# Two transfers in Pool's queue make one weight sum, and eighteen of twenty-two chunk pairs take seven products

## The chip, the cores and the metric

The kernel runs on one core of one Trainium2 chip. The metric is the device time of a run in microseconds; lower is better. The core has TensorE (PE, matrix products), VectorE (DVE), ScalarE (ACT) and GpSimd (Pool) for work on tiles, and SyncE (SP), which here only issues transfers. Each engine runs its own list of instructions in order and waits on semaphores for the others. Transfers run beside the engines on 16 DMA engines.

## The reference, cut to what matters

Two layers, each of a feed-forward network (FFN), a token mix with three kinds of attention, and another FFN, each followed by a layer norm. The change touches the first half of the FFNs only:

```python
def _swiglu(x, w1, w2):
    gt, up = jnp.split(x @ w1, 2, axis=-1)
    return (jax.nn.silu(gt) * up) @ w2
...
for l in range(DEPTH):
    x = _layer_norm(DN_ALPHA * x + 0.5 * _swiglu(x, ffn1_w1[l], ffn1_w2[l]), ln1_g[l], ln1_b[l])
    mix = _token_mix(x, w_in[l], ...)
    x = _layer_norm(DN_ALPHA * x + mix, ln2_g[l], ln2_b[l])
    x = _layer_norm(DN_ALPHA * x + 0.5 * _swiglu(x, ffn2_w1[l], ffn2_w2[l]), ln3_g[l], ln3_b[l])
```

All is fp32. There are 512 tokens of width 1024, and the hidden width is 2816, so that `w1` has 1024 x 5632 elements: 22 chunks of 128 gate columns, then 22 chunks of 128 up columns.

## The kernel before, in words

**Precision.** An fp32 operand is split into a rounded part `hi` and the rest `lo`. A product takes three matmuls: `hi` with the high part of the tokens (`xh`), `hi` with the low part (`xl`), and `lo` with `xh`. The split of a weight tile (`wsplit`, L146 and L147) is a copy on ACT, which makes `hi`, and a subtraction on DVE, which makes `lo`.

**Pairs.** An FFN works through 22 pairs f = 0 to 21, pair f being gate chunk f and up chunk f. Pairs 0 and 1 are `staged`: their weights come ahead of time, and their products run while the layer norm before them is ending. The others run in the loop in `ffn`. There are four FFNs in a run, which are called FFN0 to FFN3 here in order of time; FFN0 and FFN1 belong to the first layer.

**Plain pairs.** The pairs in `PLAIN` (0, 1, 2, 3, 4, 5 and 14) load two raw tiles of 512 KB (`wcols`), split both, and run two products of 8 steps of k with three matmuls of 128x512 each (`proj`, `mm3`, L167 to L169).

**Short pairs.** The other fifteen pairs go through `seven` and `strassen`. The gate and up columns of a chunk, each cut in two halves of k, form a 2 x 2 block matrix, and the tokens, cut in halves of k and of the 512 tokens, another. Their product takes seven block products instead of eight, which needs sums of weight blocks and sums of token blocks. A block product is four steps of k with three matmuls of 128x256 (L357). `seven` loads the raw tiles `rg` and `ru` in SP's queue (L286, L287) and makes four sums of 128x512 on DVE: L293 `x1[h1] = ru[h1] + ru[h2]`, L294 `x1[h2] = x1[h1] - rg[h1]`, L295 `x2[h1] = rg[h1] - ru[h1]`, L296 `x2[h2] = rg[h2] - x1[h2]`. Then `x1`, `x2` and half of `ru` are split (L298 on ACT and L299 on DVE for the first two, L300 and L301 for the half, into `dh` and `dl`), and `rg` is split by `wsplit`. The token sums are made once in each FFN (`token_sums`, L314 to L320), after pair 2. `strassen` gathers the results from PSUM with five DVE rows of 128x256 (L368 to L376), and `evac` applies the gate with a tanh on ACT and two DVE rows of 128x512 (L335, L336).

**Buffers.** Raw tiles share three buffers (tag `raw`). `x1` and `x2` share the tag `ws` with two buffers. `dh` and `dl` have one each. The split tiles go round a fixed rotation in `unit`: three buffers in `wt`, twice two in `more`, twice two in `w1p`; a counter runs on from FFN to FFN. `evac` has three buffers `t`.

**Order.** PE and Pool run in the order of the program text (`manual_schedule`). The instructions of ACT, DVE and SP are put in order by a scheduler. Pool's queue holds in each FFN the four stores of the residual `x_sp` (L382) at the start and its four loads `xa` (L415) after the loop, and between FFNs arithmetic of the layer norm and the attention.

**Around it.** In FFN0 two transfers of 1.5 MB (`bvec`) are issued in the loop. After the loop, the second weight `w2` is multiplied row by row (`rows_ln`), with the layer norm at its end.

Of the kernel before, what the change touches and what calls it, by code (L numbers as in the profile page):

```python
# [9 lines left out]
F32 = mybir.dt.float32  # L10
# [3 lines left out]
OP = mybir.AluOpType  # L14
# [4 lines left out]
P = 128  # L19
S, D, F = 512, 1024, 2816  # L20
KD, KF, NB = D // P, F // P, S // P
# [43 lines left out]
def body(tc, a, out, depth=DEPTH):  # L65
    nc = tc.nc
# [48 lines left out]
    def wraw(shape=None):  # L115
        return wt.tile(list(shape or [P, KD, P]), F32, name="raw", tag="raw", bufs=3)
# [11 lines left out]
    nx = K()  # L128
    nx.pool = nx.w1 = None

    def unit():

        if nx.pool:
            pl, nb = nx.pool, 4
        else:
            seq = [(wt, 3)] * 3 + [(more.pool, 2)] * 2 * bool(more.pool) + [(nx.w1, 2)] * 2 * bool(nx.w1)
            more.n += 1
            pl, nb = seq[more.n % len(seq)]
        return [pl.tile([P, KD, P], F32R, name=n, tag=n, bufs=nb) for n in ("hi", "lo")]

    def wsplit(raw, n=KD, step=None):
        hi, lo = unit()
        step = step or n
        for i in range(0, n, step):
            c = slice(i, i + step)
            nc.scalar.activation(hi[:, c], raw[:, c], AF.Copy)  # L146
            nc.vector.tensor_tensor(lo[:, c], raw[:, c], hi[:, c].bitcast(F32), op=OP.subtract)  # L147
        return hi, lo
# [123 lines left out]
        return pts  # L272

    NTAIL = 4
    PLAIN = (0, 1, 2, 3, 4, 5, 14)

    def ffn_first(w1):
        return [wcols(w1, c) for c in (0, F, P, F + P)]
# [1 line left out]
    def seven(w1, f):  # L280

        v = w1.rearrange("(k p) f -> p k f", p=P)
        rg, ru = wraw(), wraw()
        nc.sync.dma_start(rg, v[:, :, f * P:(f + 1) * P])  # L286
        nc.sync.dma_start(ru, v[:, :, F + f * P:F + (f + 1) * P])  # L287
        ug, u1, u2 = wsplit(rg), unit(), unit()
        ud = [nx.w1.tile([P, 4, P], F32R, name=n, tag=n) for n in ("dh", "dl")]
        h1, h2 = slice(0, 4), slice(4, 8)  # L290
        x1, x2 = [nx.w1.tile([P, KD, P], F32, name="ws", tag="ws", bufs=2) for _ in range(2)]
        tt = nc.vector.tensor_tensor
        tt(x1[:, h1], ru[:, h1], ru[:, h2], op=OP.add)  # L293
        tt(x1[:, h2], x1[:, h1], rg[:, h1], op=OP.subtract)  # L294
        tt(x2[:, h1], rg[:, h1], ru[:, h1], op=OP.subtract)  # L295
        tt(x2[:, h2], rg[:, h2], x1[:, h2], op=OP.subtract)  # L296
        for (hi, lo), x in ((u1, x1), (u2, x2)):
            nc.scalar.activation(hi, x, AF.Copy)  # L298
            tt(lo, x, hi.bitcast(F32), op=OP.subtract)  # L299
        nc.scalar.activation(ud[0], ru[:, h2], AF.Copy)  # L300
        tt(ud[1], ru[:, h2], ud[0].bitcast(F32), op=OP.subtract)  # L301
        return ug, u1, u2, ud
# [20 lines left out]
    def ffn(l, w1, w2, which, xap, xa, wts, pend, done_prev, last, nxt):  # L323


        st = K()
        NA = KF - NTAIL

        def hpart(f):
            return (st.ha, st.hb)[f >= NA][:, f - NA * (f >= NA)]  # L330

        def evac(f, pg, pu):
            t = st.lnp.tile([P, S], F32, name="t", tag="t", bufs=3)
            nc.scalar.activation(t, pg, AF.Tanh, scale=0.5)
            nc.vector.scalar_tensor_tensor(t, t, 1.0, pg, op0=OP.add, op1=OP.mult)  # L335
            nc.vector.tensor_tensor(hpart(f), t, pu, op=OP.mult)  # L336
# [10 lines left out]
        def strassen(f, ws):  # L347
            (ug, u1, u2, ud), (t1, t2, t3, t4) = ws, st.t
            ga, pa, pb = ps(name="pg"), ps(name="pu"), ps(name="pv")
            p_, r_, s_ = [(xh[:, k:k + 4, c], xl[:, k:k + 4, c]) for k, c in ((0, H1), (4, H1), (4, H2))]  # L350

            def prod(o, w, k0, x, first=True):
                for k in range(4):
                    hi, lo = w[0][:, k0 + k], w[1][:, k0 + k]
                    vh, vl = x[0][:, k], x[1][:, k]
                    for i, (wx, vx) in enumerate(((hi, vh), (hi, vl), (lo, vh))):
                        nc.tensor.matmul(o, wx, vx, start=first and k == 0 and i == 0, stop=k == 3 and i == 2,  # L357
                                         skip_group_check=True)

            tt = nc.vector.tensor_tensor  # L360
            prod(ga[:, H1], ug, 0, p_)
            prod(ga[:, H2], u1, 0, t1, False)
            sn = st.w1p.tile([P, S], F32, name="sn", tag="sn", bufs=2)
            nc.scalar.activation(sn, ga, AF.Copy)
            prod(pa[:, H1], u1, 4, t2)
            prod(pa[:, H2], u2, 0, t3, False)
            v = st.w1p.tile([P, S], F32, name="v", tag="v", bufs=2)
            tt(v[:, H1], pa[:, H1], sn[:, H1], op=OP.add)  # L368
            tt(v[:, H2], pa[:, H2], v[:, H1], op=OP.add)
            prod(pb[:, H1], ud, 0, t4)  # L370
            u = hpart(f)
            tt(u[:, H1], pb[:, H1], v[:, H2], op=OP.add)
            tt(u[:, H2], sn[:, H2], v[:, H2], op=OP.add)
            prod(ga[:, H1], ug, 4, r_, False)
            prod(ga[:, H2], u2, 4, s_, False)
            tt(ga[:, H2], ga[:, H2], v[:, H1], op=OP.add)  # L376
            evac(f, ga, u)

        pts = staged(wts, pend)
# [8 lines left out]
        st.ha = fa.tile([P, NA, S], F32, name="ha")  # L388
        st.w1p = nx.w1 = pool("w1p", side="right", reuse_waits="tile")
        evac(0, pts[0], pts[1])  # L390
        evac(1, pts[2], pts[3])
        for f in range(2, KF):
            if after and f in (10, 14):
                i = after.pop()
                nc.sync.dma_start(bvec[i], bsml[i, :, None, :].to_broadcast([H, P, TLEN]))
            if f == KF - 1:
                for k, n in enumerate(("hi", "lo")):
                    h_parts(k, wt.tile([P, KD, P], F32R, name=n, tag=n, bufs=3)
                            .rearrange("p (a b) c -> p a (b c)", a=2))
            if f not in PLAIN:  # L400
                strassen(f, seven(w1, f))
                continue
            wg, wu = wcols(w1, f * P), wcols(w1, F + f * P)
            pg, pu = ps(name="pg"), ps(name="pu")
            proj(pg, wg)
            proj(pu, wu)
            evac(f, pg, pu)
            if f == 2:
                token_sums(st)
# [952 lines left out]
```

## Time and profile before

| | |
|---|---|
| median of the runs | 2524.89 us |
| lowest and highest | 2524.28 and 2526.05 us |
| profiled execution | 2527.23 us |
| its span on the core | 2525.5 us |
| mean granted clock of PE | 0.995 |
| busy: PE, DVE, ACT, Pool | 98%, 64%, 43%, 8% |
| DMA, SP's queue and Pool's queue | 35.3% and 2.2% of the 16 engines' time |

The span runs from the first to the last instruction of the profiled execution. Names such as `L357` are lines of the kernel file. In a row of the profile `out<-in` gives the tiles by the names of the program, and x24 says that 24 instructions stand in one row. "Idle before" is the time that an engine stood still just before a row, with the engine and instruction that released it. PEclk is the clock that was granted to PE, 1.00 being full speed.

### The profile page before, as it was taken

The numbers are of one execution on the slowest core, as the hardware profiler recorded it, in microseconds if no ns is written. First come the engines' busy times: TensorE is split into PE (matmuls) and PEld (weight loads), VectorE is DVE, ScalarE is ACT, GpSimd is POOL, SyncE is SP. The second block draws the span as 40 slices with busy tenths as digits, with TensorE's granted clock in tenths as the row PEclk, the third lists the DMA queues.
The fourth block names the chain that finished last, engine by engine and source line by source line (L and its number), as shares of the span: only waits on it lengthen the run. The fifth ranks groups of instructions, "written<-read, shape, count | busy, mean of one in ns | idle before, by whom it ended". The sixth has DMA issues, their size and how long they took to land.

```text
span 2525.5 us, 39561 instructions
## 1 busy us (share of the span) xinstructions
PE 2486.2 (98%) x15259; PEld 2173.6 (86%) x15259; DVE 1616.5 (64%) x3309; ACT 1078.2 (43%) x2107; POOL 202.1 (8%) x403
## 2 busy tenths in 40 slices
PE   6999999999999999999999999999999999999998
PEld 6899888788888888998889998877888888899987
DVE  5688445677753458884377883556776534788844
ACT  3344333566642333443333442345766332334432
POOL 0000000133300000000000000001333000000000
PEclk8999999999999999999999999999999999999999
DMA  5333543632243342434332343435321434323441
GB/s 194 119 109 101 159 111 100 180 100 75 65 125 101 121 134 67 118 91 169 118 108 82 103 158 110 124 114 157 97 76 43 146 100 135 112 76 109 134 134 59
DMA packets 379948, 286.10 MB, mean 113 GB/s; under 512 B 17912, under 2 KB 351800, under 8 KB 379760
## 3 DMA queue, kind: packets, MB, share of 16 engines
q1 hardware_dynamic: 374000, 262.61, 35.3%
q0 software_dynamic: 5760, 20.97, 2.2%
q8 instruction: 120, 1.97, 0.3%
q14 instruction: 68, 0.56, 0.1%
HBM read 256.22 MB, written 17.88 MB: 109 GB/s over the span
## 4 chain that ended last, share of the span: by engine, by line
PE 47%; DVE 1%; DMA 1%; ACT 1%; issue 0%; POOL 0%; DVEq 0%; SPq 0%; POOLq 0%; ACTq 0%
PE pg L357 7%; PE pu L357 3%; PE acc L181 3%; PE acc L180 3%; PE acc L182 3%; PE pj L167 3%; PE pj L168 3%; PE pj L169 3%; PE pv L357 2%; PE gate L167 1%; PE gate L168 1%; PE gate L169 1%; PE brp L169 1%; PE brp L168 1%; PE brp L167 1%; PE sN L881 1%
## 5 line engine op out<-in xcount | busy, mean ns | idle before, releaser
L147 DVE TENSOR_TENSOR lo<-raw,hi 128x1024 fp32r<-128x1024 f32 (+2 forms) x354 | 416.0, 1181 | 541.2 <-ACT hi L146 531.7
L146 ACT ACTIVATE hi<-raw 128x1024 fp32r<-128x1024 f32 (+2 forms) x354 | 359.8, 1024 | 733.4 <-PE acc L181 225.4
L167 PE MATMUL pj<-xh,hi 128*128 128x512 f32 (+1 forms) x720 | 267.2, 371 | 0.1
L168 PE MATMUL pj<-xl,hi 128*128 128x512 f32 (+1 forms) x720 | 254.9, 354 | 2.5 <-DVE xl L227 2.5
L169 PE MATMUL pj<-xh,lo 128*128 128x512 f32 (+1 forms) x720 | 254.8, 354 | 0.0
L180 PE MATMUL acc<-hi,hs 128*128 128x512 f32 x640 | 249.5, 390 | 0.0
L182 PE MATMUL acc<-lo,hs 128*128 128x512 f32 x640 | 249.1, 389 | 0.0
L181 PE MATMUL acc<-hi,hs 128*128 128x512 f32 x640 | 249.0, 389 | 0.0
L357 PE MATMUL pg<-xh,lo 128*128 128x256 f32 x720 | 203.8, 283 | 0.0
L357 PE MATMUL pg<-xl,hi 128*128 128x256 f32 x720 | 203.8, 283 | 0.0
L357 PE MATMUL pg<-xh,hi 128*128 128x256 f32 x720 | 203.7, 283 | 0.0
L298 ACT ACTIVATE hi<-ws 128x1024 fp32r<-128x1024 f32 x120 | 126.1, 1059 | 162.4 <-DVE ws L294 65.3
L299 DVE TENSOR_TENSOR lo<-ws,hi 128x1024 fp32r<-128x1024 f32 x120 | 145.8, 1219 | 33.9 <-ACT hi L298 33.8
L169 PEld LDWEIGHTS pj<-xh,lo 128*128 128x128 f32 x720 | 136.4, 189 | 19.6
L167 PEld LDWEIGHTS pj<-xh,hi 128*128 128x128 f32 x720 | 136.8, 190 | 15.3 <-issue 3.1
L168 PEld LDWEIGHTS pj<-xl,hi 128*128 128x128 f32 x720 | 137.1, 190 | 14.6 <-DVE xl L227 3.4
L182 PEld LDWEIGHTS acc<-lo,hs 128*128 128x128 f32 x640 | 120.1, 188 | 25.0
L180 PEld LDWEIGHTS acc<-hi,hs 128*128 128x128 f32 x640 | 120.1, 188 | 24.8
L181 PEld LDWEIGHTS acc<-hi,hs 128*128 128x128 f32 x640 | 120.1, 188 | 24.7
L357 PEld LDWEIGHTS pg<-xh,hi 128*128 128x128 f32 x720 | 138.2, 192 | 0.3
L357 PEld LDWEIGHTS pg<-xl,hi 128*128 128x128 f32 x720 | 138.2, 192 | 0.3
L357 PEld LDWEIGHTS pg<-xh,lo 128*128 128x128 f32 x720 | 138.2, 192 | 0.0
(309 smaller groups left out, 6005.4 us busy)
## 6 DMA issues: line engine op xcount, KB each, us to landing
raw<-in_ffn_w_dram SPq DMA_DIRECT2D x264, 512.0 KB, 3.8
raw<-in_w_in_dram SPq DMA_DIRECT2D x56, 512.0 KB, 3.9
raw<-in_w_gate_dram SPq DMA_DIRECT2D x48, 512.0 KB, 4.0
x_sp<-xa POOLq DMA_DIRECT2D x24, 512.0 KB, 5.8
ks<-hl SPq DMA_DIRECT2D x96, 128.0 KB, 2.4
xa<-x_sp POOLq DMA_DIRECT2D x16, 512.0 KB, 5.0
raw<-in_w_out_dram SPq DMA_DIRECT2D x16, 512.0 KB, 3.5
tab<-bvec SPq DMA_DIRECT2D x16, 256.0 KB, 4.3
```

The source lines that it names most:

```text
L146: nc.scalar.activation(hi[:, c], raw[:, c], AF.Copy)
L147: nc.vector.tensor_tensor(lo[:, c], raw[:, c], hi[:, c].bitcast(F32), op=OP.subtract)
L167: nc.tensor.matmul(o, hi[:, k], vh, start=first, stop=False)
L168: nc.tensor.matmul(o, hi[:, k], vl, start=False, stop=False)
L169: nc.tensor.matmul(o, lo[:, k], vh, start=False, stop=last)
L180: nc.tensor.matmul(o, sh(k)[:, t], hi[:, c], start=k == 0, stop=False)
L181: nc.tensor.matmul(o, sl(k)[:, t], hi[:, c], start=False, stop=False)
L182: nc.tensor.matmul(o, sh(k)[:, t], lo[:, c], start=False, stop=k == nk - 1)
L298: nc.scalar.activation(hi, x, AF.Copy)
L299: tt(lo, x, hi.bitcast(F32), op=OP.subtract)
L357: nc.tensor.matmul(o, wx, vx, start=first and k == 0 and i == 0, stop=k == 3 and i == 2, skip_group_check=True)
L881: nc.tensor.matmul(o[:, 0:nb].rearrange("p k b j -> p (k b j)"), q, kx[:, 2 * b0:2 * (b0 + nb)].rearrange("p a b -> p (a b)"), start=i == ...
```

## The change

The sum L293 is no longer made on DVE. Pool issues two transfers for it: the first loads half h1 of the up columns straight from `w1` into `x1[h1]`, and the second loads half h2 to the same place and adds it on arrival. The second waits for the first, and L295 (the former L294) waits for the second. The raw tile `ru` is still loaded in SP's queue, since the other sums need it.

`PLAIN` becomes (0, 1, 2, 3), so that pairs 4, 5 and 14 take seven products too: 18 short pairs in each FFN. `x1` keeps the tag `ws` with two buffers for itself, `x2` gets a tag `wd` with one buffer, and `evac` has two buffers `t`. All lines behind L293 have a number that is higher by one in the new file.

```diff
-    PLAIN = (0, 1, 2, 3, 4, 5, 14)
+    PLAIN = (0, 1, 2, 3)
...
-        x1, x2 = [nx.w1.tile([P, KD, P], F32, name="ws", tag="ws", bufs=2) for _ in range(2)]
+        x1, x2 = [nx.w1.tile([P, KD, P], F32, name=n, tag=n, bufs=b) for n, b in (("ws", 2), ("wd", 1))]
+        nc.gpsimd.dma_start(x1[:, h1], v[:, h1, F + f * P:F + (f + 1) * P])
+        nc.gpsimd.dma_start(x1[:, h1], v[:, h2, F + f * P:F + (f + 1) * P], accum_op=OP.add)
         tt = nc.vector.tensor_tensor
-        tt(x1[:, h1], ru[:, h1], ru[:, h2], op=OP.add)
         tt(x1[:, h2], x1[:, h1], rg[:, h1], op=OP.subtract)
...
-            t = st.lnp.tile([P, S], F32, name="t", tag="t", bufs=3)
+            t = st.lnp.tile([P, S], F32, name="t", tag="t", bufs=2)
```

## Prediction

> **What bounds the kernel now.** I read the page first, then the waits of TensorE (PE), then the chain of waits, windows over one FFN, and the rows of VectorE (DVE), ScalarE (ACT) and Pool where the change touches them.
>
> ```profile
> PE 2486.2 (98%) x15259; PEld 2173.6 (86%) x15259; DVE 1616.5 (64%) x3309; ACT 1078.2 (43%) x2107; POOL 202.1 (8%) x403
> q1 hardware_dynamic: 374000, 262.61, 35.3%
> q0 software_dynamic: 5760, 20.97, 2.2%
> ```
>
> PE is busy for 98% of the span. The only long wait of PE, by the view of its waits, is one in the first FFN (FFN0; I call the four FFN0 to FFN3):
>
> ```profile
> PE pg L167 <- ACT hi L146: 13.7, 1, 13.7
> PE pg L357 <- DVE lo L299: 0.6, 1, 0.6
> ```
>
> So a shorter pair shortens the run as long as its weights are ready in time. The chain of waits inside FFN2 has nothing but PE in it. These are pieces of it; columns are start, duration, what.
>
> ```profile
> 1340.31 0.23 PE pu L167
> ...
> 1345.07 0.23 PE pu L167
> ...
> 1352.95 5.76 PE pg L357 x48
> ...
> 1363.03 5.76 PE pg L357 x48
> ```
>
> The first two rows lie seven steps of k apart, 4.76 us, so one step (three matmuls) takes 0.68 us, and a plain pair of 16 steps takes 10.88 us. The piece of 5.76 us joins the end of one short pair to the start of the next, so the last two rows lie one short pair apart: 10.08 us. PE is therefore the bound, but the helper engines have little room beside it, as the windows show (columns: stretch, its length, then busy time of PE, PEld, DVE, ACT and POOL, clock, DMA share, GB/s).
>
> ```profile
> 40.00:55.50 15.50, 1.81 (x6) 0.39 (x3) 6.02 (x9) 4.14 (x5) 0.00 (x0) 0.50 0.33 102
> 55.50:60.00 4.50, 4.25 (x10) 2.94 (x11) 4.50 (x5) 4.50 (x5) 0.00 (x0) 0.55 0.53 200
> 1345.70:1426.40 80.70, 80.70 (x674) 80.70 (x673) 67.14 (x105) 36.83 (x47) 0.00 (x0) 1.00 0.36 105
> ```
>
> ```profile
> L301 DVE TENSOR_TENSOR dl<-raw,dh 128x512 fp32r<-128x512 f32 x7 | 4.8, 685 | 0.8 <-ACT dh L300 0.8
> ```
>
> In the third window PE works through eight short pairs (80.64 us). DVE, by the group row of the same window, makes seven (one L301 per pair): 67.14 / 7 = 9.6 us of work a pair, and it stands idle for the other 13.5 us. It falls 80.7 − 7 × 10.08 = 10.1 us behind PE in this stretch, without a stall above 0.6 us. Pair 14, which is plain today, then gives it back its lead.
>
> **The change, part by part.**
>
> *Twelve pairs become short.* Pairs 4, 5 and 14 of each of the four FFNs go from 10.88 to 10.08 us: 12 × 0.80 = 9.6 us less on PE. The raw loads of a pair are the same two in both forms.
>
> *One sum leaves DVE.* These rows are DVE's within one pair (start, duration, line, names, wait in brackets):
>
> ```profile
> 1369.40 0.69 DVE L293 TENSOR_TENSOR ws<-raw 128x512 f32<-128x512 f32 x1 [0.37 <-DMA raw<-in_ffn_w_dram]
> 1370.01 0.68 DVE L295 TENSOR_TENSOR ws<-raw 128x512 f32<-128x512 f32 x1
> ...
> 1374.62 0.42 DVE L372 TENSOR_TENSOR ha<-pv,v 128x256 f32<-128x256 f32 x1
> 1374.96 0.41 DVE L373 TENSOR_TENSOR ha<-sn,v 128x256 f32<-128x256 f32 x1
> 1375.29 2.35 DVE L299 TENSOR_TENSOR lo<-ws,hi 128x1024 fp32r<-128x1024 f32 x2
> 1377.56 0.42 DVE L376 TENSOR_TENSOR pg<-pg,v 128x256 f32<-128x256 f32 x1
> ...
> 1379.94 0.69 DVE L293 TENSOR_TENSOR ws<-raw 128x512 f32<-128x512 f32 x1 [0.48 <-DMA raw<-in_ffn_w_dram]
> ```
>
> By the starts, a 128x512 row takes 0.61 us, a 128x256 row 0.34, a 128x1024 row 1.14 (half of 1377.56 − 1375.29). The removed L293 is worth 0.6, so a pair needs 9.0 us of DVE, 1.08 less than PE's 10.08. The period of DVE here is 1379.94 − 1369.40 = 10.54, so it idles about 1 us in each pair, mostly on raw data; L293 alone waited for it 38 times:
>
> ```profile
>   DMA raw<-in_ffn_w_dram: 28.8, 38
> ```
>
> That wait does not leave with L293: its place as first reader of the gate columns is taken by the next row (L294, L295 in the new numbering), which also needs a raw tile that was loaded into a buffer just freed.
>
> *The transfers that take its place.* Per pair Pool issues a plain load of 256 KB and, when that has landed, an adding one of 256 KB. The first waits until its buffer is free, which is when DVE has made the `lo` of the pair two before. So there is a chain C from that `lo` to L295 two pairs on: issue, landing, issue, landing. The trace has these neighbours (the DMA view: KB each, us to landing; then two rows of the view by source of L415, Pool's issue and its landing times):
>
> ```profile
> raw<-in_ffn_w_dram SPq DMA_DIRECT2D x264, 512.0 KB, 3.8
> x_sp<-xa POOLq DMA_DIRECT2D x24, 512.0 KB, 5.8
> xa<-x_sp POOLq DMA_DIRECT2D x16, 512.0 KB, 5.0
> raw<-in_w_br_c_dram SPq DMA_DIRECT2D x16, 256.0 KB, 3.4
> raw<-in_w_br_a_dram SPq DMA_DIRECT2D x16, 256.0 KB, 2.8
> ```
>
> ```profile
> L415 POOL DMA_DIRECT2D xa<-x_sp x16: 527/534/545, 244.3 to 2398.4; - x16
> DMA to landing us min/median/max: 3.5/5.0/7.7
> ```
>
> Low end: two transfers of this very shape at SP's median, 2 × 2.8 to 2 × 3.4, so 5.6 to 6.8 us. High end: two of Pool's largest median, 2 × 5.8 = 11.6. No row shows a transfer that adds. It has to read and write its destination, so 256 KB of it touch as much as Pool's 512 KB rows (5.0 to 5.8; I take 5.3), and I put the plain half between SP's 3.1 and Pool's 5.3, at 4.2. That gives C = 9.5, with both ends kept for the range.
>
> The Trainium skill, "DMA: Bandwidth & Descriptors", section on the anatomy of one DMA on the gpsimd path, gives about 2.0 us plus bytes over 436 GB/s. By it 256 KB take 2.6 us, and two with their issues some 6.3 (an estimate), which would stall nothing and is the second rival. Against it, it would give 3.2 us for 512 KB, where Pool's rows above have 5.0 and 5.8.
>
> What covers C is the DVE work that stands between that `lo` and that L295 in the order in which the scheduler puts the changed kernel's instructions. In pairs 7 to 19 of FFN0, the steady part, this differs from pair to pair. Three times it is only two splits of 128x1024 (2.28), three rows of 128x512 (1.83) and three of 128x256 (1.02), 5.2 us rounded up; twice it is 6.5 us; eight times 9.2 to 9.6. The other three FFNs have the same pattern. Waits per FFN at C = 9.5: 3 × 4.3 + 2 × 3.0 = 18.9 us. In the eight other pairs the Pool chain is just covered, and the raw wait of about 1 us stays: 8. Together 27. Against it stand 13 × 1.08 = 14 us of slack, and the lead: 10.1 us were given up before without a stall. The lead at pair 6 is now smaller, since pairs 4 and 5 now cost DVE sums and splits of their own; I take 7. So PE waits for 27 − 21 = 6 us in each FFN, 24 in all. This stall ends at C = 8.3; from there to 10.3 each us of C costs 4 × 5 = 20 us.
>
> *Restart in FFN0.* Here `lo` and `hi` of pair 2 wait behind `hi` of a later pair, whose raw tile is late (ACT, DVE and PE from the timeline):
>
> ```profile
> 47.24 1.06 ACT L146 ACTIVATE hi<-raw 128x1024 fp32r<-128x1024 f32 x1 [5.30 <-DMA raw<-in_ffn_w_dram]
> 53.47 2.95 ACT L146 ACTIVATE hi<-raw 128x1024 fp32r<-128x1024 f32 x3 [5.17 <-DMA raw<-in_ffn_w_dram]
> ```
>
> ```profile
> 54.56 3.50 DVE L147 TENSOR_TENSOR lo<-raw,hi 128x1024 fp32r<-128x1024 f32 x3 [4.23 <-ACT hi L146]
> ```
>
> ```profile
> 55.52 0.79 PE L167 MATMUL pg<-xh,hi 128*128 128x512 f32 x1 [13.71 <-ACT hi L146]
> ...
> 56.97 0.79 PE L169 MATMUL pg<-xh,lo 128*128 128x512 f32 x1 [0.23 <-DVE lo L147]
> ...
> 59.66 0.40 PE L169 MATMUL pg<-xh,lo 128*128 128x512 f32 x1
> ```
>
> In the changed order `hi` of pair 2 comes directly behind the one of 47.24, so at about 48.3, and its `lo` at about 50.4 to 51.5 instead of 55.7 to 56.9: 5.4 us less. What is late next is pair 4, whose up tile is the late one and which now also needs its Pool chain: between 0 and 4 us, I take 2.
>
> *Start of FFN2.* The rotation of weight buffers is shifted by the three extra pairs, and the scheduler now puts `lo` of pair 2 behind the first evacuations and the token sums, which were behind it before:
>
> ```profile
> 1302.24 1.28 DVE L336 TENSOR_TENSOR ha<-t,pj 128x512 f32<-128x512 f32 x2 [1.56 <-PE pj L169]
> 1303.45 4.62 DVE L314 TENSOR_TENSOR ha<-xh,xl 128x1024 f32<-128x1024 f32 x4
> 1307.99 2.35 DVE L147 TENSOR_TENSOR lo<-raw,hi 128x1024 fp32r<-128x1024 f32 x2
> ```
>
> These start when the staged pairs end on PE (1302.2). `lo` then comes at 1307.99 + 1.2 = 1309.2, and PE, after its first two matmuls (0.5 us), waits 6.5 us. FFN0 shows what an idle PE pays at restart: from 55.52 to 59.66 matmuls start 0.43 us apart instead of 0.23, at a clock of 0.50, about 2.1 us lost. With it the cost is 8.6; without, 6.5; the trace has only the longer idle of 13.7 us, and I take 8.6. In FFN1 and FFN3 `lo` stays in front, and I see no stall. The Trainium skill, "TensorE: Matmul & The Clock Gate", Part 1, says that half rate returns after an idle window of about 3.4 us; by it 6.5 us are enough, the sum would be the same, and the trace agrees for 13.7.
>
> *Costed at nothing.* The third `t` buffer: `t` of a pair is read out two pairs before it is written again, 20 us. The single `wd`: its next writer stands behind its `lo` on the same engine. Pool's queue in the FFN holds the 36 new transfers, after the four stores of `x_sp` and before the four loads of `xa`; those loads wait for DVE's last pair anyway. DMA load: 512 KB more per 10.08 us are 52 GB/s on top of 105, where q1 and q0 together take 37.5% of the DMA time; raw loads may get longer (0 to 1 us a pair), and I take 0 since the raw wait is already in the sum.
>
> *Sum*, against the profiled execution's own 2527.23 us: −9.6 − 5.4 + 2 + 8.6 + 24 = +19.6, so 2546.8. The median of the runs is 2.3 below the profiled execution, so the forecast is 2544.5.
>
> **The rivals.**
>
> *Pool's chain is short (other side).* If C stays below 8.3, the 24 us are gone: 2527.23 − 4.4 − 2.3 = 2520.5. With pair 4 in time and no clock loss in FFN2 it is 2516.4. For it speak SP's 2.8 and 3.4 us for the same shape; against it Pool's own 5.0 and 5.8, and that the second half has to read what it adds to. It decides at C = 8.3.
>
> *Pool's chain is long.* At C = 11.6 the short places wait 3 × 6.4 + 2 × 5.1 = 29.4, and the other eight 1 (if the waits before cover them) to 2.3 each: 37.4 to 47.8, less 21, times 4 = 66 to 107 us. The time would be 2586 to 2627. For it speaks that Pool's maximum is 7.7; against it that Pool's rows are twice as large.
>
> *The transfers don't unload DVE.* If raw waits are what sets DVE's period, the removed 0.6 us turns into idle time, so the slack is 13 × 0.6 = 7.8 us smaller in each FFN, 31 in all: at the forecast's C 2576, at C = 8.3 2552. For it speak the 38 waits above; against it that a later DVE also frees raw tiles no sooner than PE needs them, so that the slower stream sets the period.
>
> **How the numbers follow.** No change can be told below 0.2%, 5 us. Chain between 8.3 and 10.3: 0.40, likeliest, 2544.5, its own range 2525 to 2565. Short chain: 0.30, 2516 to 2525, split by the 2519.8 bound. Long chain: 0.15, 2565 to 2627. Raw-bound DVE: 0.15, 2552 to 2576. Faster: 0.22, nearly all from the short chain. Same: 0.18, the rest of it and the lower edge of the forecast's. Slower: 0.60. The range runs from 2516 to 2600 and leaves out half of the long chain and a little at the lower end.
>
> **What would show it.** PE's plain group loses 12 × 48 matmuls and L357's line (L358 then) gains 12 × 84. The landing times of L292 and L293 give C directly. L295 on DVE waits for a DMA in about five pairs of each FFN for 3 us or more, and PE's waits list `pg` or `pv` behind `lo` or `dl` with some 24 us. Before pair 2, FFN0's wait falls from 13.7 to about 8, and FFN2 has a new one of about 6.5 with a clock of 0.5 behind it. The forecast is wrong if C is under 8.3 or over 10.3, if the lead is not 7, or if the order in FFN2 doesn't stall PE.

## The result, and the profile after

The changed kernel takes 2620.66 us (median of 5 runs, 2617.04 to 2626.56), the kernel before 2524.76 on the same occasion. The ratio is 1.0381, with a 95% interval of 1.0369 to 1.0394: it is slower by 96 us. The profiled execution took 2617.04 us, with a span of 2615.3 us, 89.8 us more than before.

Rows of the page after: busy time by engine, the two DMA queues, and issues with size and time to landing.

```profile
PE 2514.9 (96%) x15691; PEld 2210.9 (85%) x15691; DVE 1644.2 (63%) x3369; ACT 1095.9 (42%) x2143; POOL 350.2 (13%) x547
...
q1 hardware_dynamic: 374000, 262.61, 34.2%
q0 software_dynamic: 49536, 58.73, 10.6%
...
raw<-in_ffn_w_dram SPq DMA_DIRECT2D x264, 512.0 KB, 3.8
ws<-in_ffn_w_dram POOLq DMA_DIRECT2D x144, 256.0 KB, 4.7
```

PE is no longer busy nearly all the time. The waits of PE after (sum in us, times, longest) name ACT and DVE where before there was one long wait in FFN0:

```profile
PE pg L358 <- ACT sn L365: 45.5, 44, 2.4
PE pv L358 <- DVE dl L302: 10.8, 12, 5.4
PE pg L167 <- ACT hi L146: 7.7, 1, 7.7
PE pg L169 <- DVE lo L147: 7.6, 2, 6.6
PE pg L358 <- DVE lo L300: 6.8, 3, 3.0
```

Behind them stand the waits of DVE after. L295 is the second sum (L294 before), which is now the first that reads the gate tile, and which also reads what the transfers made; L296 is the first that reads the up tile.

```profile
DVE ws L295 <- DMA ws<-in_ffn_w_dram: 80.5, 29, 5.2
DVE ws L295 <- DMA raw<-in_ffn_w_dram: 61.1, 36, 4.6
DVE wd L296 <- DMA raw<-in_ffn_w_dram: 36.3, 30, 13.3
```

In 65 of 72 pairs L295 waits, sometimes for Pool's transfers, sometimes for the raw tile. Before, L293 waited 28.8 us in all. One chain in FFN2, from DVE's rows and Pool's (start, duration): the split that frees the buffer, the two issues, and L295.

```profile
1388.08 1.22 DVE L300 TENSOR_TENSOR lo<-ws,hi 128x1024 fp32r<-128x1024 f32 x1
...
1397.91 0.69 DVE L295 TENSOR_TENSOR ws<-ws,raw 128x512 f32<-128x512 f32 x1 [2.63 <-DMA ws<-in_ffn_w_dram]
```

```profile
1389.59 0.77 POOL L292 DMA_DIRECT2D ws<-in_ffn_w_dram  x1 [9.93 <-DVE lo L300]
1393.24 1.29 POOL L293 DMA_DIRECT2D ws<-in_ffn_w_dram  x1 [2.88 <-DMA ws<-in_ffn_w_dram]
```

The buffer is free at 1389.3, and L295 runs at 1397.91: 8.6 us. DVE's other work in between ends after 6.0, and it waits for the rest.

How such a wait reaches PE shows in FFN1. L295 waits for its transfers, so L377, the last of the five rows that gather an earlier pair's results, is late. ACT's tanh (L335) waits for L377, and the copy `sn` (L365) stands behind the tanh in ACT's order. PE waits for `sn`:

```profile
1019.10 0.69 DVE L295 TENSOR_TENSOR ws<-ws,raw 128x512 f32<-128x512 f32 x1 [3.07 <-DMA ws<-in_ffn_w_dram]
...
1022.72 0.42 DVE L377 TENSOR_TENSOR pg<-pg,v 128x256 f32<-128x256 f32 x1
```

```profile
1023.17 0.60 ACT L335 ACTIVATE t<-pg 128x512 f32<-128x512 f32 x1 [5.34 <-DVE pg L377]
1023.67 0.59 ACT L365 ACTIVATE sn<-pg 128x512 f32<-128x512 f32 x1
```

```profile
1024.31 0.43 PE L358 MATMUL pg<-xh,hi 128*128 128x256 f32 x1 [1.74 <-ACT sn L365]
1024.54 0.41 PE L358 MATMUL pg<-xl,hi 128*128 128x256 f32 x1
```

The last row shows a second cost. Behind this wait of 1.74 us the matmuls start some 0.21 us apart instead of 0.12, and the clock that was granted to PE is halved for 3.4 us (columns as in the windows of the prediction):

```profile
1024.50:1027.90 3.40, 3.40 (x17) 3.40 (x17) 3.10 (x5) 2.20 (x3) 1.19 (x1) 0.50 0.57 163
```

Where the 89.8 us of span lie is seen by dividing the span at the `pu` products (L167 or L358). The table gives, from PE's rows of the two traces, the time from the first `pu` matmul of pair 2 to that of pair 21, called a pair loop. If no pair waits, it is 10.88 + 8.31 + 17 × 10.08 = 190.55 us with eighteen short pairs (the up product of the first short pair starts earlier in its pair, hence 8.31).

| | FFN0 | FFN1 | FFN2 | FFN3 | sum |
|---|---|---|---|---|---|
| pair loop before | 193.8 | 193.0 | 193.0 | 193.0 | 772.8 |
| pair loop after | 224.5 | 213.5 | 205.1 | 216.3 | 859.4 |
| after, over 190.55 | 34.0 | 22.9 | 14.5 | 25.7 | 97.2 |

So the loops are 86.6 us longer, the stretch from FFN1's loop to FFN2's is 10.1 longer, FFN0's starts 4.7 earlier, and the remaining stretches change by −2.1 together: 89.9, the 89.8 but for rounding.

The 97 us of the loops are not all waiting. These are windows over the four loops after:

```profile
58.60:283.10 224.50, 203.18 (x1525) 196.02 (x1524) 162.04 (x250) 86.01 (x111) 38.10 (x38) 0.95 0.60 144
978.10:1191.60 213.50, 197.10 (x1526) 190.30 (x1525) 164.78 (x253) 86.00 (x111) 33.95 (x34) 0.99 0.56 133
1361.33:1566.42 205.09, 196.49 (x1525) 191.39 (x1524) 164.93 (x252) 86.52 (x111) 33.93 (x34) 0.98 0.59 142
2262.35:2478.63 216.28, 198.31 (x1525) 191.72 (x1524) 164.61 (x253) 86.03 (x111) 33.95 (x34) 0.98 0.55 132
```

PE stands idle for 64 us in them (859.4 less 795.1 busy), and it is busy for 33 us longer than the 762.2 that the same products take without waits. Lower granted clock is a part of these 33: at 0.95, 0.99, 0.98 and 0.98, an estimate of length times (1 − clock) gives some 20 us. Before, the clock was 1.00 in all four loops. It falls behind waits, but whether PE would have waited instead at full clock is not shown.

### The profile page after: what moved, and what is told of

The parts are those of the page before. It is cut to its first block, busy times and chain, and to the rows that moved or that the text cites. A ratio compares the mean times of both kernels' runs of the same rounds, so it can differ in the third digit from the quotient of the medians.

```text
span 2615.3 us, 40817 instructions
## 1 busy us (share of the span) xinstructions
PE 2514.9 (96%) x15691; PEld 2210.9 (85%) x15691; DVE 1644.2 (63%) x3369; ACT 1095.9 (42%) x2143; POOL 350.2 (13%) x547
## 3 DMA queue, kind: packets, MB, share of 16 engines
q1 hardware_dynamic: 374000, 262.61, 34.2%
q0 software_dynamic: 49536, 58.73, 10.6%
## 4 chain that ended last, share of the span: by engine, by line
PE 64%; DMA 14%; DVE 10%; issue 8%; ACT 2%; POOL 1%; SPq 0%; DVEq 0%; POOLq 0%; ACTq 0%
DMA raw<-in_ffn_w_dram 10%; PE acc L181 6%; PE acc L180 6%; PE acc L182 6%; PE pg L358 4%; DMA ws<-in_ffn_w_dram 4%; PE pj L167 4%; PE pj L168 4%; PE pj L169 4%; PE gate L167 3%; PE gate L168 3%; PE gate L169 3%; PE pu L358 2%; DVE lo L300 2%; PE brp L168 2%
## 5 line engine op out<-in xcount | busy, mean ns | idle before, releaser
L358 PE MATMUL pg<-xh,hi 128*128 128x256 f32 x864 | 255.8, 296 | 45.6 <-ACT sn L365 45.5
L167 PE MATMUL pj<-xh,hi 128*128 128x512 f32 (+1 forms) x720 | 267.5, 372 | 0.1
L358 PE MATMUL pg<-xh,lo 128*128 128x256 f32 x864 | 250.1, 289 | 0.0
L358 PE MATMUL pg<-xl,hi 128*128 128x256 f32 x864 | 249.9, 289 | 0.0
L358 PEld LDWEIGHTS pg<-xh,hi 128*128 128x128 f32 x864 | 171.3, 198 | 56.0 <-ACT sn L365 55.6
L358 PEld LDWEIGHTS pg<-xl,hi 128*128 128x128 f32 x864 | 171.6, 199 | 0.2
L358 PEld LDWEIGHTS pg<-xh,lo 128*128 128x128 f32 x864 | 171.3, 198 | 0.0
L358 PE MATMUL pu<-th,hi 128*128 128x256 f32 x576 | 164.6, 286 | 0.0
L358 PE MATMUL pu<-th,lo 128*128 128x256 f32 x576 | 164.5, 286 | 0.0
L358 PE MATMUL pu<-tl,hi 128*128 128x256 f32 x576 | 164.5, 286 | 0.0
L167 PEld LDWEIGHTS pj<-xh,hi 128*128 128x128 f32 x720 | 137.2, 191 | 15.3 <-issue 3.1
L335 ACT ACTIVATE t<-pg 128x512 f32<-128x512 f32 x80 | 47.7, 597 | 240.2 <-DVE pg L377 231.0
L180 PEld LDWEIGHTS acc<-hi,hs 128*128 128x128 f32 x640 | 120.1, 188 | 24.9
```

The lines of the kernel that those rows point to most:

```text
L167: nc.tensor.matmul(o, hi[:, k], vh, start=first, stop=False)
L180: nc.tensor.matmul(o, sh(k)[:, t], hi[:, c], start=k == 0, stop=False)
```

## The experiments

Theory 1 is that DVE waits for Pool's chain of two transfers (and, 1b, for raw tiles). Theory 2 is that eighteen short pairs are too many for the helper engines anyway. Theory 3 is that the transfers slow the other transfers by their traffic. In all that follows, "loss" is the sum of the four pair loops over 4 × 190.55 = 762.2.

**Eighteen pairs, the sum on DVE.**

```diff
-        nc.gpsimd.dma_start(x1[:, h1], v[:, h1, F + f * P:F + (f + 1) * P])
-        nc.gpsimd.dma_start(x1[:, h1], v[:, h2, F + f * P:F + (f + 1) * P], accum_op=OP.add)
         tt = nc.vector.tensor_tensor
+        tt(x1[:, h1], ru[:, h1], ru[:, h2], op=OP.add)
```

> Eighteen short pairs, but the first sum is made on DVE again and Pool issues nothing for it. Theory 1 (the waits for Pool's transfers and the raw waits that they bring cost the 96 us): most of the loss goes, 2515 to 2545 us; DVE needs 9.6 us a pair plus about 1 us of raw waits against PE's 10.08, so up to 5 us of stall in each FFN remain. Theory 2 (eighteen short pairs almost in a row are too many for the helper engines, whoever makes the sum): 2590 us or more.

Measured: 2529.19 us, ratio 1.0020 (1.0011 to 1.0030). The loss is 10.8 us, 6.8 of it in FFN0; FFN1 and FFN3 run at full rate but for 0.9 us each. Theory 2 is out. DVE with four sums, 9.6 us a pair, keeps up with PE, and 91 of the 96 us come with the transfers.

**Fifteen pairs, the sum by transfers.**

```diff
-    PLAIN = (0, 1, 2, 3)
+    PLAIN = (0, 1, 2, 3, 4, 5, 14)
```

> The transfers and the buffers of the change, but PLAIN as before, fifteen short pairs. Theory 1 (the transfers make DVE wait, some 2 us in each short pair): slower than before; each FFN has 15 x 2.2 = 33 us of waits against 16 us of slack, 7 us of lead and about 7 us that plain pair 14 gives back, so 3 to 10 us of stall in each FFN, 2530 to 2565 us. Theory 2 (the number of short pairs): within 5 us of before, 2520 to 2530.

Measured: 2547.39 us, ratio 1.0089 (1.0074 to 1.0104), as theory 1 has it. The transfers cost 23 us even where three plain pairs give lead back in each FFN. DVE's waits in this kernel:

```profile
DVE ws L295 <- DMA raw<-in_ffn_w_dram: 69.7, 32, 4.8
DVE ws L295 <- DMA ws<-in_ffn_w_dram: 49.5, 17, 5.2
DVE wd L296 <- DMA raw<-in_ffn_w_dram: 20.4, 28, 2.9
```

**Without the adding transfer.** This kernel leaves half h2 out of the sum.

```diff
-        nc.gpsimd.dma_start(x1[:, h1], v[:, h2, F + f * P:F + (f + 1) * P], accum_op=OP.add)
```

> The changed kernel without the second, adding transfer; the sum holds one half only, so the computation is incomplete. DVE's work and the raw loads stay, and the chain from the lo to L295 falls from about 9 to about 4.2 us. Theory 1a (the chain sets the loss): the 17 to 22 us of waits for ws in each FFN go, and only raw waits remain, 2525 to 2545 us. Theory 1b (the raw tiles set DVE's period, since the gate tile is now needed first): raw waits take the place of the others, 2580 us or more.

Measured: 2533.87 us, ratio 1.0033 (1.0020 to 1.0046), inside what 1a expected and far from the 2580 of 1b. The loss is 17.5 us, 12.7 of it in FFN0. Half the chain costs nearly nothing. The waits of DVE show why this is not simply "no waits" (L294 here is L295 of the changed kernel, L295 is L296):

```profile
DVE ws L294 <- DMA raw<-in_ffn_w_dram: 79.4, 59, 5.2
DVE wd L295 <- DMA raw<-in_ffn_w_dram: 11.5, 10, 5.8
DVE ws L294 <- DMA ws<-in_ffn_w_dram: 10.2, 3, 7.8
```

They add up to 101 us. DVE needs 9.0 us in a pair of 10.08, so it has to stand idle for 72 × 1.08 = 78 us in any case, and waits up to that sum cost nothing. In the changed kernel the same three rows add up to 178 us.

**The transfers beside the sum on DVE.** The transfers go to a tile `dm` that nothing reads.

```diff
+        dm = nx.w1.tile([P, 4, P], F32, name="dm", tag="dm", bufs=2)
+        nc.gpsimd.dma_start(dm, v[:, h1, F + f * P:F + (f + 1) * P])
+        nc.gpsimd.dma_start(dm, v[:, h2, F + f * P:F + (f + 1) * P], accum_op=OP.add)
         tt = nc.vector.tensor_tensor
+        tt(x1[:, h1], ru[:, h1], ru[:, h2], op=OP.add)
...
-            sn = st.w1p.tile([P, S], F32, name="sn", tag="sn", bufs=2)
+            sn = st.w1p.tile([P, S], F32, name="sn", tag="sn", bufs=1)
...
-            v = st.w1p.tile([P, S], F32, name="v", tag="v", bufs=2)
+            v = st.w1p.tile([P, S], F32, name="v", tag="v", bufs=1)
```

> Eighteen short pairs with the sum on DVE; both transfers are still issued by Pool, but into a tile that nothing reads (sn and v have one buffer each to make room). Theory 3 (the transfers slow the raw loads, with DMA busy at 0.57 instead of 0.35): at least 30 us slower than the kernel with eighteen pairs and no transfers, with raw landings above 5 us. Theory 1 (it is the waiting, not the traffic): within 8 us of that kernel.

Measured: 2589.89 us, ratio 1.0260 (1.0244 to 1.0275), 60.7 us above the kernel without transfers. Theory 3's expectation came true, and mine of theory 1 failed. Nothing waits for these transfers, so Pool issues them one behind the other: in FFN1 they are all out by 1079.4 us. The windows before and after that moment (busy times of PE, PEld, DVE, ACT, POOL; then clock, DMA share, GB/s):

```profile
985.00:1075.00 90.00, 83.12 (x625) 80.98 (x624) 65.63 (x102) 32.00 (x42) 26.30 (x26) 0.94 0.70 155
1075.00:1170.00 95.00, 93.16 (x771) 92.46 (x770) 87.41 (x142) 45.03 (x58) 1.75 (x2) 1.00 0.42 110
```

With the transfers under way DMA is 70% busy and DVE gets through 65.63 us of work in 90; when they are over, 87.41 in 95. The median landing of the up tiles is 5.1 us here against 4.6 in the kernel without transfers, that of the gate tiles 4.1 against 3.8. So dense traffic does slow raw loads enough to stall PE. (One buffer each for `sn` and `v` is hardly the reason: the control below has it too and is not slower for it.) Whether it does so at the changed kernel's pace (two transfers a pair) this run does not tell; the next ones do.

**A control.** The next two kernels need 4 KB of room in each partition, which one buffer each for `sn` and `v` gives (the last two edits of the diff above). Alone:

> The changed kernel with one buffer instead of two for sn and for v, which frees 4 KB a partition for the next two kernels. Each is read out several us before it is written again, so every theory expects the time of the changed kernel, 2612 to 2628 us.

Measured: 2603.94 us, ratio 1.0319 (1.0295 to 1.0343), 17 us below the changed kernel, which no theory expected. The scheduler's order on DVE, ACT and SP is the same. What gives the 17 us stays open; the next two are compared with this run, and a difference below 17 us says little by itself.

**A third buffer for `ws`.**

```diff
-        x1, x2 = [nx.w1.tile([P, KD, P], F32, name=n, tag=n, bufs=b) for n, b in (("ws", 2), ("wd", 1))]
+        x1, x2 = [nx.w1.tile([P, KD, P], F32, name=n, tag=n, bufs=b) for n, b in (("ws", 3), ("wd", 1))]
```

> As that, with a third ws buffer, so that Pool's two transfers for a pair may start one pair earlier; their number and size stay. Theory 1 (DVE waits for the chain of two transfers): the 80 us of waits at L295 for ws go, 2530 to 2570 us. Theory 3 (the traffic of the transfers slows the raw loads, and the chain is only where it shows): raw waits grow in its place, 2590 us or more.

Measured: 2555.23 us, ratio 1.0117 (1.0101 to 1.0133), 49 us below the control, as theory 1 has it. DVE's waits for the transfers fall from 82.2 us in the control to 1.8, but those for raw tiles at L295 rise from 56.2 to 94.9:

```profile
DVE ws L295 <- DMA raw<-in_ffn_w_dram: 94.9, 60, 5.1
DVE wd L296 <- DMA raw<-in_ffn_w_dram: 31.9, 20, 13.4
...
DVE ws L295 <- DMA ws<-in_ffn_w_dram: 1.8, 2, 1.6
```

**A fourth raw tile.** Every second up tile comes from a buffer of its own, so that a raw buffer is used again after four loads.

```diff
+    st_odd = [0]
...
-        rg, ru = wraw(), wraw()
+        rg = wraw()
+        st_odd[0] ^= 1
+        ru = nx.w1.tile([P, KD, P], F32, name="raw", tag="raw", bufs=1) if st_odd[0] else wraw()
```

> As the first, with four raw tiles in the ring instead of three, so that a raw load may start one tile earlier; Pool's chain stays as it is. Theory 1b or 3 (raw loads that start late or run slowly set the pace): the 97 us of raw waits at L295 and L296 mostly go, 2545 to 2580 us. Theory 1 (the chain alone sets the pace): the waits move to ws, 2595 us or more.

Measured: 2593.34 us, ratio 1.0272 (1.0256 to 1.0287), 11 us below the control, between the two expectations. The raw wait at L295 (L299 here) is gone, but the one for the transfers has grown from 82.2 us in the control:

```profile
DVE ws L299 <- DMA ws<-in_ffn_w_dram: 128.1, 62, 4.8
DVE wd L300 <- DMA raw<-in_ffn_w_dram: 26.1, 26, 9.4
...
DVE ws L299 <- DMA raw<-in_ffn_w_dram: 1.1, 1, 1.1
```

One instruction needs both, so each wait hides behind the other, and removing one uncovers the other.

**Both at once.** The half that the transfers write is a tile of its own (`xa1`, three buffers), the other half `xb1` has one; the two together need the room that `ws` had.

```diff
+        xa1, xb1, x2 = [nx.w1.tile([P, k, P], F32, name=n, tag=n, bufs=b)
+                        for n, k, b in (("ws", 4, 3), ("wb", 4, 1), ("wd", KD, 1))]
...
-        for (hi, lo), x in ((u1, x1), (u2, x2)):
-            nc.scalar.activation(hi, x, AF.Copy)
-            tt(lo, x, hi.bitcast(F32), op=OP.subtract)
+        for (hi, lo), x, c in ((u1, xa1, h1), (u1, xb1, h2), (u2, x2, slice(0, KD))):
+            nc.scalar.activation(hi[:, c], x, AF.Copy)
+            tt(lo[:, c], x, hi[:, c].bitcast(F32), op=OP.subtract)
```

> The changed kernel with both waits covered at once: the half of x1 that the transfers write is a tile of its own with three buffers (2 KB each, the other half one buffer; its split takes two rows of 512 instead of one of 1024 on ACT and DVE), and there are four raw tiles in the ring. The transfers stay. Theory 1 with 1b (the waits for the chain and for raw tiles add up, and each alone only hands over to the other): both rows of waits at L295 fall below 30 us in all and the time to 2525 to 2550 us. Theory 3 (the traffic itself): raw and ws waits stay above 80 us and the time above 2560.

Measured: 2527.52 us, ratio 1.0013 (1.0003 to 1.0022). The pair loops are 196.7, 190.6, 190.6 and 190.6 us: at PE's rate everywhere but in FFN0. DVE does not wait at the second sum at all; of the raw waits one row is left, and 12.2 us of it are one wait in FFN0 (L301 here is L296 of the changed kernel).

```profile
DVE wd L301 <- DMA raw<-in_ffn_w_dram: 23.0, 13, 12.2
```

```profile
q0 software_dynamic: 49536, 58.73, 10.7%
```

The traffic is the same as in the changed kernel. Theory 3 is therefore not the cause there: at two transfers a pair, with a spare buffer on either side, the traffic stalls nothing.

The waits go with the size of the loss too. DVE's waits for DMA at these two sums, less the 78 us that DVE is idle anyway, against the loss in the pair loops (the shifted rotation comes next):

| kernel | waits | less 78 | loss |
|---|---|---|---|
| changed | 177.9 | 100 | 97 |
| control | 163.9 | 86 | 82 |
| fourth raw tile | 155.3 | 77 | 73 |
| third `ws` | 128.6 | 51 | 40 |
| no adding transfer | 101.1 | 23 | 18 |
| shifted rotation | 155.8 | 78 | 71 |
| both | 23.0 | none | 6 |

This is in part bookkeeping: where DVE waits for little else, a loop lasts as long as DVE's work and these waits together. That the waits are the cause is shown by the runs that take them away. The run with idle transfers doesn't fit into the table: DVE makes four sums there and has about 35 us of slack, its waits for raw tiles are 58.2 us, and the loss is 70. What makes up the rest there was not worked out.

**The rotation of the weight buffers.**

```diff
         nx.w1 = None
+        more.n += 4
```

> The changed kernel with the counter of the weight buffers moved on by four after each FFN, so that each FFN starts at the same place of the rotation as in the kernel before; nothing else. The scheduler then puts the lo of pair 2 in FFN2 ahead of the token sums again. Expected: PE's 6.6 us wait at the start of FFN2 and its restart at half clock go, 8 to 11 us less than the changed kernel, 2608 to 2614 us. If the rotation were no cause: 2617 us or more.

Measured: 2577.75 us, ratio 1.0207 (1.0182 to 1.0232). It is 43 us below the changed kernel, four times what was expected. PE's wait of 6.6 us at the start of FFN2 is gone, and the stretch from FFN1's loop to FFN2's is 9.6 us shorter, as expected; but the pair loops are 25.9 us shorter as well. DVE waits 22 us less:

```profile
DVE ws L295 <- DMA ws<-in_ffn_w_dram: 68.9, 25, 5.6
DVE ws L295 <- DMA raw<-in_ffn_w_dram: 55.4, 36, 4.4
DVE wd L296 <- DMA raw<-in_ffn_w_dram: 31.5, 25, 13.4
```

Why the shift shortens these waits was not found.

**Versions with eighteen pairs and no transfers.** First the sum on DVE with the shifted rotation; then the same with the fourth raw tile; then that with the sum as an instruction of Pool, `nc.gpsimd.tensor_tensor(x1[:, h1], ru[:, h1], ru[:, h2], op=OP.add)`.

> Eighteen short pairs with the sum on DVE and no transfers, and the counter of the weight buffers moved on by four after each FFN. Without the stall at the start of FFN2 it should be 8 to 10 us below the kernel with eighteen pairs alone: 2518 to 2523 us, so 0 to 6 us faster than before.

> As that, with four raw tiles in the ring (sn and v with one buffer). If raw waits cause what is left of the stalls (about 10 us in the pairs of FFN0 and FFN2), 2510 to 2520 us; if FFN0's late up tile causes it, 2518 to 2523.

> As that, with the first sum made by Pool as an instruction of its own instead of by DVE: no transfers, and DVE at 9.0 us a pair. If DVE's work is what is left, 2508 to 2516 us; if Pool's sum comes later than DVE's (its rows of 128x256 take 0.63 us in the trace before, so one of 128x512 about 1.2) or disturbs DVE, 2516 to 2530.

Measured: 2519.65 us, ratio 0.9981 (0.9972 to 0.9989); 2520.21 us, 0.9986 (0.9977 to 0.9995); 2518.85 us, 0.9981 (0.9972 to 0.9989). The three cannot be told apart. All are 4 to 5.5 us faster than the kernel before, so the three additional short pairs do gain, if less than 12 × 0.8: in the first, the loops of FFN1 to FFN3 take 191.4 or 191.5 us against 193.0 before, but FFN0's takes 197.7 against 193.8. The second lies just above the range for raw waits and inside the other. Its raw waits at the sums did not get shorter, 27.5 us against 21.4 in the first. Pool's sum costs 1.8 us on average where DVE's takes 0.69, and DVE then waits for it 49 times:

```profile
L296 POOL TENSOR_TENSOR ws<-raw 128x512 f32<-128x512 f32 x72 | 130.3, 1810 | 661.6 <-DMA raw<-in_ffn_w_dram 568.6 <-PE pu L168 22.0 <-DVE v L372 22.0
```

**The transfers with both waits covered and the shifted rotation.**

> The change with both waits covered (three buffers for the half that the transfers write, four raw tiles) and with the rotation moved on by four after each FFN. If covering the two waits is all that the change lacked, 8 to 10 us less than the same without the shift of the rotation, 2516 to 2520 us, level with eighteen pairs and the sum on DVE (2519.65) or up to 3 us below it, since the pair loops of FFN1 to FFN3 were at 190.6 us against 191.4. If the shift changes the order elsewhere for the worse, 2522 or more.

Measured: 2521.75 us, ratio 0.9991 (0.9982 to 1.0000), 5.8 us less than without the shift, where 8 to 10 were expected, and so just above the range of 2516 to 2520. With the waits covered the shift acts on the start of FFN2 (6.9 us less) and hardly on the loops (1.9 us more in all), which suggests that in the changed kernel the other part of its effect came through the waits. And the transfers then give nothing over the sum on DVE (2519.65): PE is the bound in both.

## Why the prediction was right or wrong

The direction was right, and so was the kind of wait: Pool's chain makes DVE wait, and PE with it. The size was far off: 2544.5 forecast, 2620.66 measured, outside the range of 2516 to 2600. The step that failed is the sum of waits in each FFN, in which the raw waits stood at 8 us and measured 21.

- *Twelve short pairs, −9.6.* Right: with all waits covered the loops of FFN1 to FFN3 take 190.6 us against 193.0, −2.4 in each.
- *C = 9.5, as 4.2 + 5.3.* Right. The landing times in the changed kernel are, for the plain half and then for the adding one:

```profile
DMA to landing us min/median/max: 3.2/3.6/8.4
```

```profile
DMA to landing us min/median/max: 4.4/4.8/8.3
```

  The medians with two gaps of 0.3 us give 9.0 (the chain above, with 3.4 and 4.7, has 8.6); the means over all 72 are 4.3 and 5.1, which gives 10.0. The Trainium skill's formula ("DMA: Bandwidth & Descriptors", anatomy of one DMA) has 2.6 us for each; no transfer of the 144 landed as fast, and the measurement decides.
- *Waits for the chain, 18.9 us in each FFN.* Right in sum, 80.5 / 4 = 20.1, and there was some luck in it: forecast were five waits of 3.0 to 4.3 us in each FFN, measured are seven of 2.8 on average.
- *Raw waits, 8 us in each FFN.* This is the term that failed. I let the raw wait of about 1 us stay in eight pairs of eighteen and took it as hidden elsewhere, and counted none at L296. Measured are (61.1 + 36.3 − 13.3) / 4 = 21 us in each FFN, the single wait of 13.3 in FFN0 left out. The prediction calls L293 the first reader of the gate columns, but it read the up tile. L295 reads the gate tile, one load after its buffer has come free, and L296 waits for the up tile besides. In FFN2 L296 frees the buffer, SP loads the next gate tile into it, and L295 waits for that load (DVE, SP, DVE):

```profile
1404.15 0.69 DVE L296 TENSOR_TENSOR wd<-raw 128x512 f32<-128x512 f32 x1 [0.48 <-DMA raw<-in_ffn_w_dram]
```

```profile
1404.90 0.37 SPq L286 DMA_DIRECT2D raw<-in_ffn_w_dram  x1
```

```profile
1408.84 0.69 DVE L295 TENSOR_TENSOR ws<-ws,raw 128x512 f32<-128x512 f32 x1 [1.47 <-DMA raw<-in_ffn_w_dram]
```

  The loads themselves are hardly slower than before, 4.0 us against 3.8 (median) for gate tiles and 3.8 in both for up tiles: the waits come from late starts. So the sum of waits was 41 where I had 27. How much of the loss is due to the raw waits alone can't be said, since they and the waits for the chain stand in for each other.
- *Slack 14 and lead 7.* Nearly right in sum: 41 us of waits make about 20 of stall ((97.2 − 15.2 of FFN0's first pairs) / 4 = 20.5), so 21 were absorbed. That it is the slack of all eighteen pairs (18 × 1.08 = 19.4) rather than of thirteen and a lead is the simpler account. The prediction has no term for the lower clock behind the waits inside the loops; the 20 us of stall include it, some 2 to 4 us in each of FFN1 to FFN3 by the estimate above. With 21 in place of 8 for the raw waits, 41 − 21 = 20 us in each FFN and 80 in all, not 24.
- *Restart of FFN0, −5.4, then pair 4, between 0 and 4.* The first is nearly right: the first `pu` product comes 4.7 us earlier, PE's wait fell from 13.7 to 7.7, and `lo` came at 52.0. The second was wrong: pairs 4 to 6 lose 15.2 us (12.16 + 11.88 + 19.65 between `pu` products, against 8.31 + 2 × 10.08). DVE waits 13.3 us for the late up tile, and then the chain is late in turn.
- *Start of FFN2, +8.6.* Nearly right: the stretch to FFN2's loop is 10.1 us longer. PE waits 6.59 us and restarts at half rate, with 0.43 us from start to start:

```profile
1353.74 0.79 PE L169 MATMUL pg<-xh,lo 128*128 128x512 f32 x1 [6.59 <-DVE lo L147]
1354.34 0.63 PE L167 MATMUL pg<-xh,hi 128*128 128x512 f32 x1
1354.76 0.63 PE L168 MATMUL pg<-xl,hi 128*128 128x512 f32 x1
```

  So 6.6 us of idle time are enough to lose the clock, which the trace before showed only for 13.7. This agrees with the rule of the Trainium skill ("TensorE: Matmul & The Clock Gate", Part 1) that I weighed there, an idle window of about 3.4 us. The waits inside the loops don't: the 1.74 us shown above were enough as well, and the measurement decides.
- *Costed at nothing.* `t` and `wd` never show as waits of size. The added traffic I took as 0 to 1 us a raw load: the landings of 4.0 and 3.8 us and the run with both waits covered bear out a value near 0, and the run with idle transfers shows what denser traffic would do.
- *The rivals.* The long chain, at 2586 to 2627 us, has the measured time in its range but not its reason: C was 9 to 10, not 11.6. The rival in which raw waits set DVE's period named the right resource, priced at 31 us instead of about 56 (the difference of 14 us in four FFNs).

## What to carry to other kernels

When an instruction needs two inputs that both come late, removing one wait uncovers the other, so covering one pays only in part: here 49 us for the transfers and 11 for the raw tiles against the control, and 76 for both. Add up the waits of the helper engine over all its pieces of work, not only over those where the new wait is worst, and compare the sum with its whole slack: here waits minus slack gave the loss of seven kernels to within 11 us. An engine with 5% of slack is not unloaded by taking 6% of its work away if the replacement adds a chain of transfers as long as its period.

## What the runs showed of the hardware

- Waits of PE far shorter than the 13.7 us at the start of FFN0 can halve its granted clock. In the changed kernel 1.74 us were followed by a clock of 0.50 from 1024.5 to 1027.9, with 17 matmuls in the 3.4 us. Another wait of 1.74 us, up to 2309.63, was followed by 1.00 and 29 matmuls in as long, and what decides is not shown.
- An adding transfer of 256 KB takes 4.8 us (median), a plain one of the same shape in the same queue 3.6. Pool is busy for 1.29 us to issue it, 0.77 for the plain one (1.29 for both in the run with idle transfers).

```profile
L293 POOL DMA_DIRECT2D ws<-in_ffn_w_dram x72: 1275/1286/1330, 65.7 to 2444.7; - x72
```

- It is also dear in DMA time. The run without it has this row for Pool's queue:

```profile
q0 software_dynamic: 11520, 39.85, 4.8%
```

  The kernel before has 5760 packets and 2.2%, the changed one 49536 and 10.6%. So 72 plain transfers are 5760 packets (80 each), 72 adding ones 38016 (528 each). With the spans, a plain one takes (4.8% × 2532.2 − 2.2% × 2525.5) / 72 = 0.92 us of all 16 engines, an adding one (10.6% × 2615.3 − 4.8% × 2532.2) / 72 = 2.2 us. By the first queue's row, 35.3% × 2525.5 us for 262.61 MB, a raw load of 512 KB takes 1.8 us. So adding 256 KB costs the DMA engines more than loading 512 KB.
